# An encoder trunk on one core: the last two squares of a norm summed by TensorE, the norms' low parts issued one tile later, three weight blocks split earlier

## The chip, the core and the metric

The kernel runs on one core of a Trainium2 chip. The metric is the device time of one execution in microseconds. The median of three runs of the kernel before is 2935.86 us, from 2931.73 to 2937.4.

## What is computed

Two layers of an encoder on 1280 tokens of 1024 channels: layer 0 mixes tokens by grouped-query attention, layer 1 by a convolution module; each is followed by a SwiGLU feed-forward network (FFN) of width 2816. Every part starts with a norm and ends with an addition to `x`. Cut to what matters here, everything in float32:

```
def _rms_norm(x, g):
    y = x * lax.rsqrt(jnp.mean(x * x, axis=-1, keepdims=True) + RMS_EPS)
    return y * g

# layer 0
x = x + attention(_rms_norm(x, g_attn)) @ w_o
x = x + (silu(h @ w_gate0) * (h @ w_up0)) @ w_down0        # h = _rms_norm(x, g_ffn0)
# layer 1
u, v = split(_rms_norm(x, g_conv) @ w_in + b_in)
c = depthwise_conv(u * sigmoid(v)) + dw_b                  # width 31, each sequence by itself
x = x + silu(_layer_norm(c, ln_g, ln_b)) @ w_out + b_out
x = x + (silu(h @ w_gate1) * (h @ w_up1)) @ w_down1        # h = _rms_norm(x, g_ffn1)
y = _rms_norm(x, g_final)
```

## The kernel before

**Numbers in two parts.** TensorE (PE) multiplies in a shortened float32. Each float32 operand is therefore split into a high part, a cast on ScalarE (ACT, L133), and a low part, source minus high part, on VectorE (DVE, L134); a product is three matmuls, high by high, high by low and low by high. Weights come by DMA into `raw` (four buffers) and are split into `hl` (five buffers) by `weights` (L140) or, for the FFNs computed with seven products for a 2 by 2 block in place of eight, by `seven`. Such an FFN has `two_blocks` (L732 on) with the products y, z, v and x, whose operands `norm7` (L683) makes: from the normed tiles k and k + 4 the differences `t1` to `t4` (`t12`, `t34`, L718 to L721), and of those the split pairs `b` (`cut7`, L701; `b1` in `seven_right`).

**Layout.** Activations lie with channels on the partitions, in 8 tiles of 128 (NK = 8), and tokens along the free axis. The tokens are worked off in two halves: HA (0 to 639) and HB (640 to 1279); the convolution cuts at 624 (CA, CB).

**Order of the work.** The attention fills the first 620 us. Behind it PE's queue is written out by hand: `drive(main, bg, rate)` lets the main generator run one step, then the background generator `rate` steps, and so on. The stages are: w_o of HA; w_o of HB blocks 0 to 4, beside norm7 of HA for FFN0; FFN0 HA; w_o of HB blocks 5 to 7, beside the norm of HA for the convolution; conv_in HA, beside norm7 of HB and the depthwise convolution (on DVE); FFN0 HB; conv_out CA, beside the norm of HB; conv_in HB, beside the norm of CA; FFN1 CA (in groups of blocks); conv_out CB; the last group of FFN1 CA, beside norm7 of CB; FFN1 CB; the close with the final norm. The orders of DVE, ACT, GpSimd (POOL) and SyncE (SP, which issues the loads) are made by a scheduler from the order of the code and estimated readiness; each engine works its queue off strictly in order, so an instruction that waits holds up all behind it.

**A norm.** For each of the eight tiles `Total.add` squares `x` on ACT into `sq` (L633, three buffers) and POOL adds it to the running sum (L637). `factors` lets PE multiply the sum by a column of ones, `st` (L652): eight matmuls of 80 or 82 tokens by one column for the norms of a token half, six of 104 for CA and for the final norm. DVE forms the reciprocal root in a chain of tiny operations from `rs_w` (L107) to `rs_r` (L128). `spread` broadcasts it over the partitions with PE, `bc` (L661). Then `norm` (L674) scales each tile into `hf` on DVE and splits it into `hn`, tile by tile; `norm7` scales at L692. `pause(k)` between `factors` and the norm puts k steps of the background between them, and with that one or more PE blocks of the main generator between `st` and `bc`.

**Lines that the prediction uses.** `wo` (L614) are the matmuls of a w_o block, `x<-wo` (L794) the addition behind it on DVE; `pd` those of an FFN's down projection; `ci` (L941) those of conv_in; y, z, v, x the seven products (L728 to L730); `r<-y` (L744) copies on ACT of one of them; L1055 the loads for the final norm.

Of the kernel before, what the change touches and what calls it, by code (L numbers as in the profile page):

```python
# [10 lines left out]
F32 = mybir.dt.float32  # L11
F32R = mybir.dt.float32r
I32 = mybir.dt.int32
AF = mybir.ActivationFunctionType
ALU = mybir.AluOpType
# [4 lines left out]
P = 128  # L20
D = 1024
NK = D // P
# [47 lines left out]
def trunk(ctx: ExitStack, tc: tile.TileContext, a: dict):  # L70
# [24 lines left out]
    def col(ct, r):  # L95
        return cols[:, ct, r:r + 1]
# [35 lines left out]
    def split(dst_h, dst_l, src):  # L132
        S.copy(out=dst_h, in_=src)  # L133
        V.tensor_tensor(out=dst_l, in0=src, in1=dst_h.bitcast(F32), op=ALU.subtract)  # L134
# [281 lines left out]
    with tc.tile_pool(name="at", bufs=1, reuse_waits="tile") as at, \  # L416
# [33 lines left out]
        class Unit:  # L450
            def __init__(self, spec):
                self.j, self.qt0, self.nq, self.kt0, self.nk, self.h = spec
                self.g = self.j // 2
                self.w = self.nk * P
                self.s, self.nm, self.l, self.p, self.pt = {}, {}, {}, {}, {}
                self.o = None

                heads = (0, 1) if self.h is None else (self.h,)
                tiles = [(h, i) for h in heads for i in range(self.nq)]
                per = 1024 // self.w  # L460
                self.tiles = [tiles[i:i + per] for i in range(0, len(tiles), per)]
# [131 lines left out]
    def slot(name, dt=F32):  # L593
        return sp.tile([P, SLOT], dt, tag="s", name=name)
# [4 lines left out]
    def acc(name):  # L599
        return pp.tile([P, 2, 512], F32, tag="acc", name=name)  # L600

    def two(t, half):
        return t[:, :half.len].rearrange("p (c n) -> p c n", c=2)
# [18 lines left out]
    def hl_pair(name):  # L622
        return slot(name + "h", F32R), slot(name + "l", F32R)

    class Total:


        def __init__(self, ln):
            self.ln, self.tot = ln, None

        def add(self, x):
            new = sp.tile([P, SLOT], F32, tag="sq", bufs=SQUARES, name="sq")[:, :self.ln]
            S.activation(out=new, in_=x[:, :self.ln], func=AF.Square)  # L633
            if self.tot is None:
                self.tot = new
            else:
                GP.tensor_tensor(out=self.tot, in0=self.tot, in1=new, op=ALU.add)  # L637

    def stats(xs, half, eps, box, wait=2):

# [5 lines left out]
        yield from factors(tot, half, eps, box)  # L646

    def factors(tot, half, eps, box):
        tot = getattr(tot, "tot", tot)
        st = acc("st")[:, 0, :half.nst]  # L650
        for j in range(half.nst):
            PE.matmul(st[:half.w, j:j + 1], tot[:, j * half.w:(j + 1) * half.w], ones, start=True, stop=True)  # L652
        box.append(rsqrt(st[:half.w, :], (half.w, half.nst), 1.0 / D, eps))
        yield

    def spread(r, half):

        bc = acc("bc")
        for j in range(half.nst):
            c, i = divmod(j, half.per)  # L660
            PE.matmul(bc[:, c, i * half.w:(i + 1) * half.w], r[:, j:j + 1].to_broadcast([half.w, P]),  # L661
                      ident[:half.w, :half.w], start=True, stop=True)
        return bc[:, :, :half.n]

    def norm(xs, half, row, out, box=None):

        if box is None:
            box = []
            yield from stats(xs, half, RMS_EPS, box)
            yield  # L670
        bc = spread(box[0], half)
        for ct in range(NK):
            f = slot("hf")
            V.scalar_tensor_tensor(out=two(f, half), in0=two(xs[ct], half), scalar=col(ct, row), in1=bc,  # L674
                                   op0=ALU.mult, op1=ALU.mult)
            h, l = hl_pair("hn")
            split(h[:, :half.len], l[:, :half.len], f[:, :half.len])
            out.append((h, l))
            yield

    def norm7(half, row, ops, load, box, later=None):

        n = half.n
        bc = spread(box[0], half)
        for k in range(NK // 2):
            f = []
            for ct in (k, k + NK // 2):
                x = load(ct)  # L690
                f.append(slot("hf"))
                V.scalar_tensor_tensor(out=two(f[-1], half), in0=two(x, half), scalar=col(ct, row), in1=bc,  # L692
                                       op0=ALU.mult, op1=ALU.mult)
                yield
            sums = seven_right(f[0][:, :n], f[0][:, n:2 * n], f[1], n, ops)
            for pair, x in sums:
                if later is None:
                    cut7(ops, n, pair, x)
                else:
                    later.append((pair, x))  # L700
            yield  # L701

    def cut7(ops, n, pair, x):
        h, l = hl_pair("b")
        split(h[:, :2 * n], l[:, :2 * n], x[:, :2 * n])
        for i, c in zip(pair, (slice(0, n), slice(n, 2 * n))):
            ops[i].append((h[:, c], l[:, c]))

    def seven_right(b11, b12, low, n, ops):


        b21, b22 = low[:, :n], low[:, n:2 * n]
        t12, t34 = slot("t12"), slot("t34")
        t1, t2, t3, t4 = t12[:, :n], t12[:, n:2 * n], t34[:, :n], t34[:, n:2 * n]
        p1 = slot("b1", F32R)
        split(p1[:, :n], p1[:, n:2 * n], b11)
        ops[1].append((p1[:, :n], p1[:, n:2 * n]))
        V.tensor_tensor(out=t1, in0=b12, in1=b11, op=ALU.subtract)  # L718
        V.tensor_tensor(out=t2, in0=b22, in1=t1, op=ALU.subtract)
        V.tensor_tensor(out=t3, in0=b22, in1=b12, op=ALU.subtract)  # L720
        V.tensor_tensor(out=t4, in0=b21, in1=t2, op=ALU.subtract)  # L721
        cut7(ops, n, (5, 6), t12)
        return ((7, 4), t34), ((2, 3), low)

    def product(ps, left, right, first):

# [181 lines left out]
    def pause(steps):  # L908
        for _ in range(steps):
            yield  # L910

    def first(*steps):
        for g in steps:
            yield from g
# [257 lines left out]
    with tc.manual_schedule(engines={mybir.EngineType.PE}):  # L1172
        oa, ob, xa, xb, ha, hb = [], [], [], [], sevens(), sevens()
        pairs = groups(*[2] * (FF // P // 2))
        drive(heads(HA, oa))
        box, box_b = [], []
        tot_a = Total(HA.len)
        drive(attn_out(HA, oa, xa, lambda ct, x: tot_a.add(x)), heads(HB, ob))
        tot_b, take_b = taken(HB)
        drive(attn_out(HB, ob, None, take_b, range(5)),  # L1180
              first(factors(tot_a, HA, RMS_EPS, box), pause(3), norm7(HA, R_F0, ha, lambda ct: xa[ct], box)), 4)
        ob = []
        tot_a, take_a = taken(HA)
        drive(ffn(0, ha, xa, HA, pairs, None, lambda ct: take_a(ct, xa[ct])), heads(HB, ob), 2, iter(()))
        hc, u, y, box, box_a = [], [], [], [], []
        drive(attn_out(HB, ob, None, take_b, range(5, NK)),
              first(factors(tot_a, HA, RMS_EPS, box_a), pause(2), norm(xa, HA, R_CONV, hc, box_a)), 3)
        xa, later = [], []
        w = CA.len + GAP
        bg = conv_mid(u, w, box)  # L1190
        drive(conv_in(hc, HA, u),
              both(first(factors(tot_b, HB, RMS_EPS, box_b), pause(2), norm7(HB, R_F0, hb, stored(HB), box_b, later)), bg, RATE0),
              1, finish=False)
        for pair, x in sorted(later, key=lambda p: -p[0][0]):
            cut7(hb, HB.n, pair, x)
        for ct in range(NK):
            xb.append(slot("x"))
            nc.sync.dma_start(xb[ct][:, :HB.len], x_d[ct * P:(ct + 1) * P, HB.lo:HB.hi])
        drive(ffn(0, hb, xb, HB, pairs, load=True), conv_norm(box, w, CA, y), 3, bg, RATE - 1)
        xa, ha, hc = [], [], []  # L1200
        drive(conv_out(y, CA, xa), norm(xb, HB, R_CONV, hc), 2)
        spill(xb, HB)
        u, y, box = [], [], []
        w = CB.len
        bg = conv_mid(u, w, box)
        drive(conv_in(hc, HB, u), both(norm(xa, CA, R_F1, ha), bg, RATE0), 1, finish=False)
        gs = groups(4, 4, 4, 2, 4, 4)
        drive(ffn(1, ha, xa, CA, gs[:-1]), conv_norm(box, w, CB, y), 3, bg, RATE)
        xb, hb, box, rest = [], sevens(), [], []
        drive(conv_out(y, CB, xb))  # L1210
        tot, take = taken(CA)
        drive(ffn(1, ha, xa, CA, gs[-1:], None, lambda ct: take(ct, xa[ct])),
              norm7(CB, R_F1, hb, lambda ct: xb[ct], box), 3, stats(xb, CB, RMS_EPS, box))
        drive(ffn(1, hb, xb, CB, pairs, rest), final(tot, CA))
# [41 lines left out]
```

## Time and profile before

| | |
|---|---|
| median of three runs | 2935.86 us |
| the profiled execution | 2935.9 us |
| its span, first to last instruction | 2934.1 us |
| mean granted clock of TensorE | 0.987 of full speed |
| ACT busy | 40% |
| POOL busy | 16% |
| bytes moved by DMA | 438.69 MB |

The profile is of one execution. Its busy times are those of an engine's datapath; PEld is TensorE's loading of weights, which overlaps the matmuls. Rows of the timeline give the start in us from the span's start, the length, the engine, the line of the kernel, the operation, what is written and what is read, the shapes and a count; in brackets stands how long the engine sat idle before, and whose end released it. A matmul of `st` leaves two rows, as do those of `bc`. Matmuls overlap in the timeline, so that their cost is read from the distance of starts. The granted clock is that which the throttle gave TensorE, 1.00 or 0.50 at any moment here, and a number between them is a mean over a window.

### The profile page before, as it was taken

The page shows a single profiled execution, that of the slowest core. Times are in us where ns is not written, and L with a number is a line of the kernel's source. Part 1 is how long each engine was busy: PE and PEld are TensorE (multiplying, and loading weights), DVE is VectorE, ACT ScalarE, POOL GpSimd, SP SyncE. Part 2 cuts the span into 40 slices and gives each one's busy share as a digit, 9 for nine tenths or more (in the row PEclk, how much of TensorE's full clock was granted, in tenths as well). Part 3 has the DMA queues.
Part 4 walks back from the last instruction along what each step waited for, and adds up shares of the span by engine and source line. Part 5 has one row for each costly group of instructions (what it writes and reads, how often), then busy time and mean ns, then how long its engine had stood idle before and what let it go on. Part 6 is the DMA issues. An engine that isn't in the chain of part 4 may idle for free.

```text
span 2934.1 us, 47020 instructions
## 1 busy us (share of the span) xinstructions
PE 2851.1 (97%) x18573; PEld 2728.0 (93%) x18573; DVE 2281.0 (78%) x3705; ACT 1172.4 (40%) x1853; POOL 469.7 (16%) x453
## 2 busy tenths in 40 slices
PE   8989999999999999999999999999999998999997
PEld 6767888789999999999999999999999998999997
DVE  7988999967777776697998666989984438877776
ACT  4438888864433334222111243222222324333332
POOL 2445555522000001110000213010002011000000
PEclk9999999999999999899999999999999999999999
DMA  4532232146887777357666754333324422422221
GB/s 152 181 123 58 53 90 59 44 119 196 277 280 274 267 265 258 106 180 256 223 244 222 277 182 135 115 105 91 98 91 153 130 77 94 134 87 73 86 72 52
DMA packets 316326, 438.69 MB, mean 150 GB/s; under 512 B 22297, under 2 KB 244513, under 8 KB 299209
## 3 DMA queue, kind: packets, MB, share of 16 engines
q1 hardware_dynamic: 298488, 400.10, 42.5%
q0 software_dynamic: 5280, 21.42, 2.0%
q10 hardware_dynamic: 12336, 14.16, 1.4%
q8 instruction: 146, 2.39, 0.3%
q14 instruction: 76, 0.61, 0.1%
HBM read 299.46 MB, written 130.93 MB: 147 GB/s over the span
## 4 chain that ended last, share of the span: by engine, by line
PE 80%; DVE 13%; DMA 2%; issue 2%; ACT 2%; POOL 1%; DVEq 0%; ACTq 0%; SPq 0%; POOLq 0%
PE pd L614 17%; PE ci L941 8%; PE s L472 4%; PE pt L513 4%; PE co L614 4%; PE pg L614 3%; PE pu L614 3%; DVE c L982 3%; PE z L730 3%; PE z L728 3%; PE z L729 3%; PE v L729 3%; PE v L728 3%; PE v L730 3%; PE y L728 3%; PE wo L614 3%
## 5 line engine op out<-in xcount | busy, mean ns | idle before, releaser
L133 ACT CAST hl<-raw 128x1024 fp32r<-128x1024 f32 x328 | 341.0, 1049 | 691.3 <-issue 333.1
L614 PE MATMUL pd<-hh,hl 128*128 128x320 f32 (+2 forms) x2752 | 523.8, 309 | 0.7 <-DVE x L849 0.7
L134 DVE TENSOR_TENSOR hl<-raw,hl 128x1024 fp32r<-128x1024 f32 x328 | 410.4, 1253 | 139.7 <-ACT hl L133 139.2
L982 DVE SCALAR_TENSOR_TENSOR c<-u,cols,c 128x640 f32<-128x640 f32 (+1 forms) x480 | 429.2, 897 | 8.1
L614 PEld LDWEIGHTS pd<-hh,hl 128*128 128x128 f32 x2752 | 434.1, 188 | 1.2 <-DVE x L849 1.2
L849 DVE TENSOR_TENSOR x<-pd,x 128x640 f32<-128x640 f32 (+2 forms) x304 | 248.4, 821 | 118.3 <-PE pd L614 116.4
L614 PE MATMUL pd<-hl 128*128 128x320 f32 (+2 forms) x1376 | 313.9, 309 | 0.0
L637 POOL TENSOR_TENSOR sq<-sq 128x640 f32<-128x640 f32 (+2 forms) x63 | 120.5, 1913 | 847.2 <-ACT sq L633 846.3
L614 PEld LDWEIGHTS pd<-hl 128*128 128x128 f32 x1376 | 230.6, 188 | 0.0
L941 PE MATMUL ci<-hnh,hl 128*128 128x320 f32 (+2 forms) x1024 | 198.6, 314 | 1.2 <-ACT hnh L133 0.9
L484 DVE TENSOR_SCALAR_CACHE_REDUCE s<-s,r_q 128x1024 f32<-128x1024 f32 (+1 forms) x160 | 181.1, 1132 | 23.4 <-PE s L472 16.9
L134 DVE TENSOR_TENSOR pl<-pt,ph 128x512 fp32r<-128x512 f32 x272 | 186.8, 687 | 15.2 <-ACT ph L133 10.5
L506 POOL TENSOR_SCALAR p<-p,rl 128x1024 f32<-128x1024 f32 (+1 forms) x160 | 158.2, 992 | 170.5 <-DVE rl L503 130.3
L513 PEld LDWEIGHTS pt<-ident,p 128*128 128x128 f32 x1088 | 132.3, 141 | 52.7 <-DVE pl L134 17.0
L133 ACT CAST ph<-pt 128x512 fp32r<-128x512 f32 x272 | 159.5, 589 | 48.5 <-PE pt L513 41.2
L728 PE MATMUL z<-bh,hl 128*128 128x320 f32 (+1 forms) x528 | 166.2, 315 | 11.7 <-DMA hl<-w_w_up 5.2
L513 PE MATMUL pt<-ident,p 128*128 128x128 f32 x1088 | 166.2, 275 | 7.6 <-DVE pl L134 4.3
L941 PEld LDWEIGHTS ci<-hnh,hl 128*128 128x128 f32 x1024 | 168.2, 192 | 3.1 <-ACT hnh L133 3.1
L730 PE MATMUL z<-bh,hl 128*128 128x320 f32 (+1 forms) x528 | 166.4, 315 | 1.4 <-DVE hl L134 1.4
L729 PE MATMUL z<-bl,hl 128*128 128x320 f32 (+1 forms) x528 | 166.2, 315 | 0.0
L495 ACT ACTIVATE p<-s,nm 128x1024 f32<-128x1024 f32 (+1 forms) x160 | 159.2, 998 | 10.9 <-DVE s L484 7.5
L614 PE MATMUL pu<-hnh,hl 128*128 128x312 f32 x704 | 133.6, 307 | 0.0
(238 smaller groups left out, 6809.2 us busy)
## 6 DMA issues: line engine op xcount, KB each, us to landing
raw<-in_w_down_dram SPq DMA_DIRECT2D x88, 512.0 KB
raw<-in_w_gate_dram SPq DMA_DIRECT2D x66, 512.0 KB
raw<-in_w_up_dram SPq DMA_DIRECT2D x66, 512.0 KB
w_w_gate<-hl SPq DMA_DIRECT2D x33, 1024.0 KB
w_w_up<-hl SPq DMA_DIRECT2D x33, 1024.0 KB
hl<-w_w_gate SPq DMA_DIRECT2D x33, 1024.0 KB
hl<-w_w_up SPq DMA_DIRECT2D x33, 1024.0 KB
raw<-in_conv_w_in_dram SPq DMA_DIRECT2D x32, 512.0 KB
```

The source lines that it names most:

```text
L133: S.copy(out=dst_h, in_=src)
L134: V.tensor_tensor(out=dst_l, in0=src, in1=dst_h.bitcast(F32), op=ALU.subtract)
L484: V.tensor_scalar(out=s[:, c], in0=s[:, c], scalar1=r_q[self.j // 4][b][:, i, head:head + 1], scalar2=None, op0=ALU.mult, op1=ALU.min, acc ...
L495: S.activation(out=p[:, c], in_=s[:, c], func=AF.Exp, bias=nm[:, i:i + 1], scale=-1.0, accum_out=l[:, i:i + 1])
L513: PE.transpose(ps[:, n * P:(n + 1) * P], self.p[n][:, kt * P:(kt + 1) * P], ident)
L614: PE.matmul(ps[:, c, :n], wt, x[:, c * n:(c + 1) * n], start=first and k == 0 and not end and xi == 0, stop=last and k == nk - 1 and end)
L728: PE.matmul(ps, wh, h, start=first and k == 0, stop=False, skip_group_check=True)
L729: PE.matmul(ps, wh, l, start=False, stop=False, skip_group_check=True)
L730: PE.matmul(ps, wl, h, start=False, stop=k == len(right) - 1, skip_group_check=True)
L849: V.tensor_tensor(out=two(xs[ct], half), in0=pd[:, :, :n], in1=two(xs[ct], half), op=ALU.add)
L941: PE.matmul(ps[:, c, :hi - lo], wt, x[:, lo:hi], start=k == 0 and not end and xi == 0, stop=k == NK - 1 and end)
L982: V.scalar_tensor_tensor(out=c[:, :ln], in0=u[:, k:k + ln], scalar=col(ct, R_DW + k), in1=c[:, :ln], op0=ALU.mult, op1=ALU.add)
```

## The change

Five edits, line numbers of the new kernel in brackets:

- `Total` keeps the sum of squares 0 to 5, still added up by POOL, and gives squares 6 and 7 slots of their own. `factors` multiplies all three parts by the ones and lets PE add them up in PSUM: 24 matmuls for 8, and 18 for 6 (`st`, L657). This touches all nine norms that are made in this way.
- `norm` and `norm7` issue the low part of a split one tile (of norm7: one tile pair) later: `high` (L695) issues the cast and returns the subtraction (L696) as a function that is called after the next tile's scaling (`hf`, L682 and L710). In `seven_right` `t1` and `t2` come ahead of the split of `b1`.
- While the last down projection of FFN0 HA runs, `ending` calls `weights` for three w_o blocks of HB (5, 6 and 7) after its tiles 1, 3 and 5; `attn_out` takes them from `w_a`, as it already did for earlier blocks.
- The pause before the norm of HA for the convolution is 1 for 2.
- The `later` operands of norm7 of HB are cast first, all of them, and then subtracted.

```diff
     class Total:
         def __init__(self, ln):
-            self.ln, self.tot = ln, None
+            self.ln, self.parts, self.count = ln, [], 0
 
         def add(self, x):
-            new = sp.tile([P, SLOT], F32, tag="sq", bufs=SQUARES, name="sq")[:, :self.ln]
-            S.activation(out=new, in_=x[:, :self.ln], func=AF.Square)
-            if self.tot is None:
-                self.tot = new
+            self.count += 1
+            late = self.count > NK - 2
+            new = slot("sq") if late else sp.tile([P, SLOT], F32, tag="sq", bufs=SQUARES, name="sq")
+            S.activation(out=new[:, :self.ln], in_=x[:, :self.ln], func=AF.Square)
+            if late or not self.parts:
+                self.parts.append(new)
             else:
-                GP.tensor_tensor(out=self.tot, in0=self.tot, in1=new, op=ALU.add)
+                tot = self.parts[0][:, :self.ln]
+                GP.tensor_tensor(out=tot, in0=tot, in1=new[:, :self.ln], op=ALU.add)
...
     def factors(tot, half, eps, box):
-        tot = getattr(tot, "tot", tot)
         st = acc("st")[:, 0, :half.nst]
+        m = len(tot.parts) - 1
         for j in range(half.nst):
-            PE.matmul(st[:half.w, j:j + 1], tot[:, j * half.w:(j + 1) * half.w], ones, start=True, stop=True)
+            for i, part in enumerate(tot.parts):
+                PE.matmul(st[:half.w, j:j + 1], part[:, j * half.w:(j + 1) * half.w], ones, start=i == 0, stop=i == m)
...
     def norm(xs, half, row, out, box=None):
...
-        for ct in range(NK):
-            f = slot("hf")
-            V.scalar_tensor_tensor(out=two(f, half), in0=two(xs[ct], half), scalar=col(ct, row), in1=bc,
-                                   op0=ALU.mult, op1=ALU.mult)
-            h, l = hl_pair("hn")
-            split(h[:, :half.len], l[:, :half.len], f[:, :half.len])
-            out.append((h, l))
-            yield
+        past = None
+        for ct in range(NK + 1):
+            now = None
+            if ct < NK:
+                f = slot("hf")
+                V.scalar_tensor_tensor(out=two(f, half), in0=two(xs[ct], half), scalar=col(ct, row), in1=bc,
+                                       op0=ALU.mult, op1=ALU.mult)
+                h, l = hl_pair("hn")
+                now = high(h[:, :half.len], l[:, :half.len], f[:, :half.len])
+                out.append((h, l))
+            if past is not None:
+                past()
+            past = now
+            if ct < NK:
+                yield
+
+    def high(h, l, x):
+        S.copy(out=h, in_=x)
+        return lambda: V.tensor_tensor(out=l, in0=x, in1=h.bitcast(F32), op=ALU.subtract)
...
     def norm7(half, row, ops, load, box, later=None):
...
-            sums = seven_right(f[0][:, :n], f[0][:, n:2 * n], f[1], n, ops)
-            for pair, x in sums:
-                if later is None:
-                    cut7(ops, n, pair, x)
-                else:
-                    later.append((pair, x))
-            yield
+            for low in past:
+                low()
+            past = seven_right(f[0][:, :n], f[0][:, n:2 * n], f[1], n, ops, later)
+            yield
+        for low in past:
+            low()
...
+        def ending(ct):
+            take_a(ct, xa[ct])
+            if ct in (1, 3, 5):
+                c = slice((5 + ct // 2) * P, (6 + ct // 2) * P)
+                w_a.append(weights(a["w_o"][0][:, c].rearrange("(k p) c -> p k c", p=P)))
+
+        drive(ffn(0, ha, xa, HA, pairs, None, ending), heads(HB, ob), 2, iter(()))
...
-              first(factors(tot_a, HA, RMS_EPS, box_a), pause(2), norm(xa, HA, R_CONV, hc, box_a)), 3)
+              first(factors(tot_a, HA, RMS_EPS, box_a), pause(1), norm(xa, HA, R_CONV, hc, box_a)), 3)
```

PE's queue where the norm of HA for the convolution meets w_o blocks 5 and 6 of HB (`wo`): before, a whole block stands between `st` and `bc`; the rows left out are the rest of that block.

```order
L614 MATMUL wo<-ol,hl 128x320 x2
L614 MATMUL wo<-oh,hl 128x320 x2
L652 MATMUL st<-ones,sq 80x1 x8
L614 MATMUL wo<-oh,hl 128x320 x2
L614 MATMUL wo<-ol,hl 128x320 x2
...
L614 MATMUL wo<-oh,hl 128x320 x2
L661 MATMUL bc<-ident,rs_r 128x80 x8
L614 MATMUL wo<-oh,hl 128x320 x2
```

The same place after:

```order
L614 MATMUL wo<-ol,hl 128x320 x2
L614 MATMUL wo<-oh,hl 128x320 x2
L657 MATMUL st<-ones,sq 80x1 x24
L666 MATMUL bc<-ident,rs_r 128x80 x8
L614 MATMUL wo<-oh,hl 128x320 x2
```

`st` has three times as many matmuls, and `bc` stands directly behind it. Apart from the `st` at the eight other places, which have grown in the same way, PE's order is the same.

DVE's queue in norm7 of HA for FFN0, beside w_o of HB, from the first tile pair on (`t12`, `t34` the differences, `b1` and `bl` low parts, `x_` with `wo_` the addition behind w_o block 2), before:

```order
L692 SCALAR_TENSOR_TENSOR hf_8542<-x_7846,cols_105,bc_8533 128x640
L692 SCALAR_TENSOR_TENSOR hf_8544<-x_8140,cols_105,bc_8533 128x640
L134 TENSOR_TENSOR b1_8548<-hf_8542,b1_8548 128x320
L718 TENSOR_TENSOR t12_8546<-hf_8542 128x320
L720 TENSOR_TENSOR t34_8547<-hf_8544,hf_8542 128x320
L719 TENSOR_TENSOR t12_8546<-hf_8544,t12_8546 128x320
L721 TENSOR_TENSOR t34_8547<-hf_8544,t12_8546 128x320
L134 TENSOR_TENSOR bl_8556<-t12_8546,bh_8555 128x640
L134 TENSOR_TENSOR bl_8560<-t34_8547,bh_8559 128x640
L134 TENSOR_TENSOR bl_8564<-hf_8544,bh_8563 128x640
L692 SCALAR_TENSOR_TENSOR hf_8567<-x_7915,cols_105,bc_8533 128x640
L794 TENSOR_TENSOR x_8625<-wo_8576,old_8569 128x640
```

The same place after, from the third row of the above on:

```order
L732 TENSOR_TENSOR t12_8560<-hf_8556 128x320
L696 TENSOR_TENSOR b1_8564<-hf_8556,b1_8564 128x320
L733 TENSOR_TENSOR t12_8560<-hf_8558,t12_8560 128x320
L737 TENSOR_TENSOR t34_8561<-hf_8558,hf_8556 128x320
L738 TENSOR_TENSOR t34_8561<-hf_8558,t12_8560 128x320
L710 SCALAR_TENSOR_TENSOR hf_8577<-x_7915,cols_105,bc_8547 128x640
L815 TENSOR_TENSOR x_8635<-wo_8586,old_8579 128x640
L710 SCALAR_TENSOR_TENSOR hf_8641<-x_8215,cols_105,bc_8547 128x640
L696 TENSOR_TENSOR bl_8567<-t12_8560,bh_8566 128x640
L696 TENSOR_TENSOR bl_8572<-t34_8561,bh_8571 128x640
L696 TENSOR_TENSOR bl_8575<-hf_8558,bh_8574 128x640
```

The three low parts `bl` have moved behind the next pair's two scalings and behind the addition of w_o block 2.

DVE's queue in the norm of HA for the convolution, from the end of the root's chain on (`hnl` the low parts, `hl` that of a weight), before:

```order
L794 TENSOR_TENSOR x_13232<-wo_13183,old_13176 128x640
L134 TENSOR_TENSOR hl_13572<-raw_13570,hl_13572 128x1024
L674 SCALAR_TENSOR_TENSOR hf_13247<-x_7846,cols_105,bc_13238 128x640
L134 TENSOR_TENSOR hnl_13250<-hf_13247,hnh_13249 128x640
L674 SCALAR_TENSOR_TENSOR hf_13253<-x_7915,cols_105,bc_13238 128x640
L134 TENSOR_TENSOR hnl_13256<-hf_13253,hnh_13255 128x640
L674 SCALAR_TENSOR_TENSOR hf_13259<-x_7990,cols_105,bc_13238 128x640
L134 TENSOR_TENSOR hnl_13262<-hf_13259,hnh_13261 128x640
```

And after:

```order
L682 SCALAR_TENSOR_TENSOR hf_13223<-x_7846,cols_105,bc_13214 128x640
L815 TENSOR_TENSOR x_13279<-wo_13230,old_13228 128x640
L682 SCALAR_TENSOR_TENSOR hf_13284<-x_7915,cols_105,bc_13214 128x640
L134 TENSOR_TENSOR hl_13614<-raw_13612,hl_13614 128x1024
L696 TENSOR_TENSOR hnl_13226<-hf_13223,hnh_13225 128x640
L682 SCALAR_TENSOR_TENSOR hf_13290<-x_7990,cols_105,bc_13214 128x640
L696 TENSOR_TENSOR hnl_13287<-hf_13284,hnh_13286 128x640
L682 SCALAR_TENSOR_TENSOR hf_13296<-x_8065,cols_105,bc_13214 128x640
```

A tile's low part now stands behind the scaling of the next tile, and the first scaling ahead of the addition of a w_o block. In SP's queue the loads of the three w_o blocks stand where they stood.

More of the change, by code (lines that the diff above doesn't have):

```diff
@@ L686, in norm7 @@
         bc = spread(box[0], half)
+        past = []
         for k in range(NK // 2):
@@ L694, in norm7, with seven_right @@
                 yield
-            sums = seven_right(f[0][:, :n], f[0][:, n:2 * n], f[1], n, ops)
-            for pair, x in sums:
-                if later is None:
-                    cut7(ops, n, pair, x)
-                else:
-                    later.append((pair, x))
+            for low in past:
+                low()
+            past = seven_right(f[0][:, :n], f[0][:, n:2 * n], f[1], n, ops, later)
             yield
+        for low in past:
+            low()
     def cut7(ops, n, pair, x):
         h, l = hl_pair("b")
-        split(h[:, :2 * n], l[:, :2 * n], x[:, :2 * n])
         for i, c in zip(pair, (slice(0, n), slice(n, 2 * n))):
             ops[i].append((h[:, c], l[:, c]))
-    def seven_right(b11, b12, low, n, ops):
+        return high(h[:, :2 * n], l[:, :2 * n], x[:, :2 * n])
+    def seven_right(b11, b12, low, n, ops, later):
         b21, b22 = low[:, :n], low[:, n:2 * n]
@@ L714, in seven_right @@
         t1, t2, t3, t4 = t12[:, :n], t12[:, n:2 * n], t34[:, :n], t34[:, n:2 * n]
-        p1 = slot("b1", F32R)
-        split(p1[:, :n], p1[:, n:2 * n], b11)
-        ops[1].append((p1[:, :n], p1[:, n:2 * n]))
         V.tensor_tensor(out=t1, in0=b12, in1=b11, op=ALU.subtract)
         V.tensor_tensor(out=t2, in0=b22, in1=t1, op=ALU.subtract)
+        p1 = slot("b1", F32R)
+        ops[1].append((p1[:, :n], p1[:, n:2 * n]))
+        lows = [high(p1[:, :n], p1[:, n:2 * n], b11), cut7(ops, n, (5, 6), t12)]
         V.tensor_tensor(out=t3, in0=b22, in1=b12, op=ALU.subtract)
         V.tensor_tensor(out=t4, in0=b21, in1=t2, op=ALU.subtract)
-        cut7(ops, n, (5, 6), t12)
-        return ((7, 4), t34), ((2, 3), low)
+        for pair, x in (((7, 4), t34), ((2, 3), low)):
+            if later is None:
+                lows.append(cut7(ops, n, pair, x))
+            else:
+                later.append((pair, x))
+        return lows
     def product(ps, left, right, first):
@@ L1183, in trunk @@
         tot_a, take_a = taken(HA)
-        drive(ffn(0, ha, xa, HA, pairs, None, lambda ct: take_a(ct, xa[ct])), heads(HB, ob), 2, iter(()))
+        def ending(ct):
[4 more added lines that the diff above has]
+        drive(ffn(0, ha, xa, HA, pairs, None, ending), heads(HB, ob), 2, iter(()))
         hc, u, y, box, box_a = [], [], [], [], []
         drive(attn_out(HB, ob, None, take_b, range(5, NK)),
-              first(factors(tot_a, HA, RMS_EPS, box_a), pause(2), norm(xa, HA, R_CONV, hc, box_a)), 3)
+              first(factors(tot_a, HA, RMS_EPS, box_a), pause(1), norm(xa, HA, R_CONV, hc, box_a)), 3)
         xa, later = [], []
@@ L1193, in trunk @@
               1, finish=False)
-        for pair, x in sorted(later, key=lambda p: -p[0][0]):
-            cut7(hb, HB.n, pair, x)
+        for low in [cut7(hb, HB.n, pair, x) for pair, x in sorted(later, key=lambda p: -p[0][0])]:
+            low()
         for ct in range(NK):
```

## The prediction

> **What bounds the kernel now.** The page comes first: TensorE (PE) is busy for 97% of the span, so the time is PE's work plus the few places where it idles or runs at a low clock.
>
> ```profile
> PE 2851.1 (97%) x18573; PEld 2728.0 (93%) x18573; DVE 2281.0 (78%) x3705; ACT 1172.4 (40%) x1853; POOL 469.7 (16%) x453
> ```
>
> The view of waits on PE names who ends its idle times (total, times, longest). The third row is what the longer `st` is meant for; the first and the fourth are the norm7 operands; the second, a DMA, isn't touched.
>
> ```profile
> PE y L728 <- ACT b L133: 5.5, 2, 3.8
> PE z L728 <- DMA hl<-w_w_up: 5.2, 1, 5.2
> PE st L652 <- POOL sq L637: 4.3, 2, 2.9
> PE z L728 <- ACT hl L133: 3.7, 1, 3.7
> ```
>
> The view of windows over the five places that the change touches (length, then busy time of PE, PEld, DVE, ACT, POOL, then granted clock, DMA share, GB/s). In order: FFN0 HA's start beside norm7; the `st` behind w_o block 4 of HB; conv_in HA's start behind norm HA; the `st` of norm CA; FFN1 CB's start.
>
> ```profile
> 724.00:740.00 16.00, 11.61 (x58) 10.47 (x57) 14.37 (x24) 7.90 (x12) 6.57 (x2) 0.79 0.62 217
> 1160.00:1172.00 12.00, 9.13 (x60) 8.88 (x60) 5.43 (x7) 5.78 (x7) 5.61 (x4) 0.86 0.40 137
> 1186.00:1210.00 24.00, 20.92 (x88) 17.29 (x87) 15.07 (x27) 7.72 (x9) 2.43 (x3) 0.64 0.26 68
> 2220.00:2240.00 20.00, 18.56 (x127) 18.30 (x126) 14.49 (x26) 3.06 (x4) 5.79 (x5) 0.91 0.53 171
> 2450.00:2480.00 30.00, 22.25 (x126) 20.81 (x126) 27.13 (x37) 15.66 (x22) 6.85 (x4) 0.83 0.39 122
> ```
>
> What PE loses in a row is its idle time plus the clock's shortfall times the length: 4.4 + 0.21 × 16 = 7.8; 2.9 + 1.7 = 4.6; 3.1 + 8.6 = 11.7; 1.4 + 1.8 = 3.2; 7.8 + 5.1 = 12.9. That is 40.2 us: the most that the edits can win.
>
> **The sum of squares: more PE work at nine places.** The timeline shows an `st` and the matmul behind it (start, length, ... x rows; a matmul of this form leaves two rows), for a norm 80 tokens wide and for a conv norm 104 wide.
>
> ```profile
> 692.51 1.24 PE L652 MATMUL st<-ones,sq 128*80 128x1 f32 x16
> 693.61 0.54 PE L614 MATMUL wo<-oh,hl 128*128 128x320 f32 x2
> 2479.53 1.17 PE L652 MATMUL st<-ones,sq 128*104 128x1 f32 x12
> 2480.57 0.40 PE L728 MATMUL y<-b,hl 128*128 128x328 f32 x1
> ```
>
> Eight matmuls take between 1.10 us (to the next start) and 1.24 (their length): I take 1.15; the six wide ones between 1.04 and 1.17: 1.10. Three parts take three times as long, so the addition is twice that: seven places × 2.3 = 16.1 and two × 2.2 = 4.4, together **+20.6** (the bounds are 19.6 and 22.0). PE is busy in front of and behind all nine, so nothing hides it. POOL loses 18 additions; it is 16% busy, and they count only where `st` waited for them.
>
> **What three parts do to the clock.** PE alone, in stretches on the 3.41 us grid on which the clock changes (length, busy, granted clock, DMA share, GB/s):
>
> ```profile
> 692.00:695.41 3.41, 3.41 (x33) 1.00 0.36 133
> 1659.63:1663.04 3.41, 1.68 (x12) 1.00 0.85 348
> 1663.04:1666.45 3.41, 3.04 (x21) 1.00 0.88 284
> 2226.24:2229.65 3.41, 1.97 (x22) 1.00 0.89 279
> 2229.65:2233.06 3.41, 3.41 (x15) 0.50 0.43 114
> 1202.24:1205.65 3.41, 3.41 (x22) 0.50 0.02 5
> 2228.14 1.33 PE L652 MATMUL st<-ones,sq 128*82 128x1 f32 x16 [1.44 <-POOL sq L637]
> 1202.47 2.21 PE L652 MATMUL st<-ones,sq 128*80 128x1 f32 x16
> ```
>
> The first row holds an `st` of today's length and keeps its clock. A stretch with 1.68 busy keeps the clock; one with 1.97 busy, of which the `st` (seventh row) is about 1.2, loses it. So `st` rows don't seem to count as work: without them that stretch has 0.8 us. The sixth row says the same: PE is busy throughout, 2.2 us of it `st`, and the stretch doesn't raise the clock for the rest. An `st` of 3.45 us covers most of one stretch wherever it falls: the uncovered part drops below 0.8 us at about half of the positions, and below 1.68 at nearly all. I take three in four. One stretch at 0.50 loses half of 3.41: 1.7. At the six places that keep the clock today: 6 × 0.75 × 1.7 = **+7.7** (0 if `st` does count, 20.5 if each drop lasts two stretches).
>
> The Trainium skill, "TensorE: Matmul & The Clock Gate", section "HAM oscillation — how this bites in real kernels", gives the rule "no PE-idle gaps >~3.4µs". By that rule a busy `st` drops nothing, and the sum would be 7.7 us lower; the trace disagrees, since a wait of 1.44 us with an `st` behind it was enough at 2226.
>
> **Waits that go, and what is late next.** Squares 6 and 7 no longer pass through POOL. At 2228.14 the wait of 1.44 goes, with a little of its low clock: **−1.6**.
>
> ```profile
> 1160.83 1.57 POOL L637 TENSOR_TENSOR sq<-sq 128x640 f32<-128x640 f32 x1 [0.85 <-ACT sq L633]
> 1162.43 0.74 ACT L633 ACTIVATE sq<-x 128x640 f32<-128x640 f32 x1 [1.68 <-POOL sq L637]
> 1167.24 1.58 PE L652 MATMUL st<-ones,sq 128*80 128x1 f32 x16 [2.87 <-POOL sq L637]
> 1204.72 0.16 DVE L107 TENSOR_SCALAR rs_w<-st 80x8 f32<-80x8 f32 x1 [3.53 <-PE st L652]
> 1207.92 0.16 DVE L128 SCALAR_TENSOR_TENSOR rs_r<-rs_t,rs_r 80x8 f32<-80x8 f32 x1
> 1195.55 0.83 DVE L134 TENSOR_TENSOR hnl<-hf,hnh 128x640 fp32r<-128x640 f32 x1 [0.79 <-ACT hnh L133]
> 1197.95 0.82 DVE L134 TENSOR_TENSOR hnl<-hf,hnh 128x640 fp32r<-128x640 f32 x1 [0.79 <-ACT hnh L133]
> ```
>
> At 1167.24 the sums come one after the other (1.57 after a square of 0.74). With the sixth addition over at 1162.4 and the last square free of POOL's buffers, `st` starts when w_o is through, 2.87 earlier. But with one pause less, `bc` stands directly behind `st`: all of PE's queue, w_o blocks 6 and 7 and conv_in, waits for the reciprocal root, whose chain on DVE takes 3.36 us from the fourth to the fifth row (a w_o subtraction in it would make it 5). That idle time costs a stretch at half clock, 1.7. In return norm HA's tiles no longer wait for their own cast: the last two rows show one tile per 2.40 us, 0.79 of it waiting; all eight pace conv_in's first part, 8 × 0.79 = 6.3. Sum: −2.87 + 3.36 + 1.7 − 6.3 = **−4.1** (from +2.2, if PE was paced by the clock alone, to −8.5, if DVE's chain finds cover).
>
> **FFN0 HA's start (724).** DVE is 14.37 of 16 busy there, so a reordered DVE queue counts one to one.
>
> ```profile
> 707.23 1.56 DVE L134 TENSOR_TENSOR bl<-t,bh 128x640 fp32r<-128x640 f32 x2 [0.27 <-ACT bh L133]
> 709.45 0.87 DVE L692 SCALAR_TENSOR_TENSOR hf<-x,cols,bc 128x640 f32<-128x640 f32 x1
> 710.24 0.82 DVE L794 TENSOR_TENSOR x<-wo,old 128x640 f32<-128x640 f32 x1
> 709.77 1.05 ACT L133 CAST hl<-raw 128x1024 fp32r<-128x1024 f32 x1 [1.31 <-PE wo L614]
> 736.62 0.39 PE L728 MATMUL x<-bh,hl 128*128 128x320 f32 x1 [0.51 <-DVE x L794]
> ```
>
> In the new DVE order the addition `x<-wo` stands ahead of the three low parts of the first tile pair, and PE's w_o block ends only at about 709.7 (fourth row, a cast that waits for the same block). Before, DVE spent the time from 707.23 on the low parts (first row), ahead of the addition; now it idles some 2.2 us there, and by my walk along the new order some 1.4 more behind a weight's low part whose cast is late. Nothing gives that back, since PE still waits for DVE in the last row, at 736.62: **+3.5** (0 to +7.8).
>
> **FFN1 CB's start (2450).** PE's `z` waits for the weight's low part on DVE and starts again at 2466.39.
>
> ```profile
> 2462.98 1.04 ACT L133 CAST hl<-raw 128x1024 fp32r<-128x1024 f32 x1
> 2466.39 0.64 PE L730 MATMUL z<-bh,hl 128*128 128x328 f32 x1 [1.40 <-DVE hl L134]
> 1669.87 0.74 ACT L633 ACTIVATE sq<-c 128x640 f32<-128x640 f32 x1
> 1670.52 0.41 ACT L744 COPY r<-y 128x320 f32<-128x320 f32 x1
> ```
>
> Now that cast (first row) and its partner stand ahead of the operand's, and DVE takes the weight's low parts before the last `bl`s: `z` could go at 2463.4 or so, 3.0 earlier; less half a microsecond for POOL still adding there: **−2.5** (0 to −12.9). In FFN0 HB the two last squares now stand together on ACT, one of 0.74 ahead of the copy of `r` (rows three and four): **+0.7**.
>
> **At nothing.** The w_o weights issued early: SP's queue has their loads where they stood, behind the same raw buffers, and only their casts could move. `cut7` of `later`: DVE and ACT work beside the FFN's matmuls, hidden by them; without that cover the eight low parts come up to eight casts of 0.74 late. The two squares' own slots: 0 to 1 us if a slot were missing.
>
> **Sum.** 20.6 + 7.7 − 1.6 − 4.1 + 3.5 − 2.5 + 0.7 = +24.3. The profiled execution took 2935.9 with its span of 2934.1, and the median of the three runs is 2935.86, so both give **2960**.
>
> **The rivals.** (1) The clock holds at the six places: 2960 − 7.7 = 2952. For it: an `st` as it is drops no clock at six of nine places. Against: the stretch at 2226. By the quoted rule of the skill it would come out so. (2) The other side: the reordered norms keep DVE from waiting for ACT, so that PE never starves at the five places, and the clock holds there. All 40.2 go: 2935.9 + 20.6 − 40.2 = 2916. It decides as soon as 20.6 + 5.9 = 26.5 of the 40.2 go with the clock held, or 34 with the drops. For it: 0.79 idle per tile. Against: DVE is itself full in the windows at 724 and 2450, and an order of its queue gives it no time. (3) Half of the 40.2 goes and the clock holds: 2935.9 + 20.6 − 20.1 = 2936. (4) Each drop lasts two stretches, as with 6.83 us at 727.79 today: 20.5 in place of 7.7, 2973.
>
> ```profile
> 727.79:734.62 6.83, 5.62 (x19) 0.50 0.32 116
> ```
>
> That the w_o edit does nothing is already in the sum; the other edits are in the order of the queues.
>
> **The numbers.** What a measurement can tell from no change is about 0.2%, 5.9 us. Chances: the forecast 0.53, (1) 0.15, (2) 0.09, (3) 0.11, (4) 0.12. Slower is the forecast with (1) and (4): 0.80; same 0.11; faster 0.09. The range 2940 to 2976 takes in (1), (4) and the bounds of the terms; it leaves out (2) and the lower part of (3).
>
> **What would show it.** Nine `st` of 3.3 to 3.6 us (408 rows where there were 136); stretches of clock 0.50 behind most of those at 692, 1687, 1773, 1838, 2390 and 2480; no wait of `st` for POOL; a wait of `bc` for `rs_r` of 3 to 5 us near 1170; norm tiles every 1.6 us; x of FFN0 HA some 3.5 us later against its block's start. The forecast is wrong if `st` takes far less than three times as long, if the clock stays at 1.00 behind it, or if PE's losses at 724, 1186 and 2450 shrink by over 26 us.

## The result, and the profile after

The changed kernel takes 2965.44 us (median of four runs, 2956.74 to 2968.06) against 2936.63 for the kernel before: 1.0095 times as long, 95% interval 1.007 to 1.012. It is slower by 28.8 us, by the interval 21 to 35; 2960, or +24.3, was forecast.

The page of the changed kernel (busy time, share of the span, instructions): PE is busy for 28.0 us more with 272 more rows, POOL for 33.4 us less; DVE and ACT have nearly what they had.

```profile
PE 2879.1 (97%) x18845; PEld 2759.8 (93%) x18845; DVE 2275.1 (77%) x3705; ACT 1171.2 (40%) x1853; POOL 436.3 (15%) x435
```

The waits of its PE (total, times, longest). No `st` waits for POOL any more. In its place `y` waits for the low part of `b1` (first row), at FFN0 HA's and FFN1 CB's start, and `bc` waits for the root.

```profile
PE y L750 <- DVE b L696: 10.3, 3, 4.0
PE y L749 <- ACT b L695: 5.4, 2, 3.0
...
PE bc L666 <- DVE rs_r L128: 3.6, 1, 3.6
...
PE z L749 <- DMA hl<-w_w_gate: 3.0, 1, 3.0
```

An `st` of the new kernel, and the stretches of low clock behind five of the six `st` that had none before (length, PE busy, granted clock, DMA share, GB/s). 48 rows take 3.83 us to the next matmul here, since their last part already runs at the low clock; where the clock is full they take 3.4 (third and fourth row).

```profile
1693.64 3.97 PE L657 MATMUL st<-ones,sq 128*80 128x1 f32 x48
1697.47 0.88 PE L614 MATMUL pd<-hh,hl 128*128 128x320 f32 x2
...
691.49 3.53 PE L657 MATMUL st<-ones,sq 128*80 128x1 f32 x48
694.89 0.54 PE L614 MATMUL wo<-oh,hl 128*128 128x320 f32 x2
```

```profile
1696.53:1703.36 6.83, 6.83 (x31) 0.50 0.00 0
1788.69:1792.10 3.41, 3.41 (x15) 0.50 0.17 44
1856.95:1863.78 6.83, 6.83 (x31) 0.50 0.24 69
2416.74:2420.15 3.41, 3.41 (x16) 0.50 0.15 10
2508.90:2515.73 6.83, 6.83 (x28) 0.50 0.01 2
```

PE is busy all through them, so that busy time does not show this loss; the granted clock does. They are eight stretches of 3.41 us at half speed, 27.3 us, a loss of 13.7.

Where the time went is read from the same matmul in both traces. The lag is its start after less its start before; the profiled executions took 2935.9 and 2966.58.

| up to (start before, start after) | lag | step | forecast |
|---|---|---|---|
| first `st` (692.51, 691.49) | -1.0 | | |
| first y of FFN0 HA (723.64, 725.00) | 1.4 | +2.4 | 2.3 rows + 1.3 clock |
| its first x (736.62, 742.66) | 6.0 | +4.7 | +3.5 |
| a y of FFN0 HB (1313.95, 1320.54) | 6.6 | +0.5 | -4.1 + 2 × 2.3 rows = +0.5 |
| a v of it (1584.42, 1588.95) | 4.5 | -2.1 | 0 |
| a y of it, behind `st` (1691.59, 1703.72) | 12.1 | +7.6 | 2.3 + 1.3 + 0.7 = 4.3 |
| conv_in HB (1817.47, 1833.45) | 16.0 | +3.9 | 2.3 + 1.3 |
| a `pg` of FFN1 CA (1932.61, 1953.86) | 21.3 | +5.3 | 2.2 + 1.3 |
| a `pg` behind the `st` of CB (2241.29, 2263.37) | 22.1 | +0.8 | 2.3 - 1.6 |
| a `pg` behind the next (2398.16, 2424.62) | 26.5 | +4.4 | 2.3 + 1.3 |
| a v of FFN1 CB (2484.25, 2516.07) | 31.8 | +5.4 | -2.5 + 2.2 + 1.3 = 1.0 |
| end of the span (2934.1, 2964.8) | 30.7 | -1.1 | 0 |

### The profile page after: what moved, and what is told of

Its sections match the earlier page's. It is cut to its first block, busy times and chain, and to the rows that moved or that the text cites. A ratio compares the mean times of both kernels' runs of the same rounds, so it can differ in the third digit from the quotient of the medians.

```text
span 2964.8 us, 47538 instructions
## 1 busy us (share of the span) xinstructions
PE 2879.1 (97%) x18845; PEld 2759.8 (93%) x18845; DVE 2275.1 (77%) x3705; ACT 1171.2 (40%) x1853; POOL 436.3 (15%) x435
## 4 chain that ended last, share of the span: by engine, by line
PE 88%; DVE 8%; DMA 2%; issue 1%; ACT 1%; POOL 0%; DVEq 0%; ACTq 0%; SPq 0%; POOLq 0%
PE pd L614 19%; PE ci L962 8%; PE pg L614 5%; PE pu L614 5%; PE s L472 4%; PE pt L513 4%; PE co L614 4%; PE wo L614 3%; PE z L751 3%; PE z L749 3%; PE z L750 3%; PE v L749 3%; PE v L750 3%; PE v L751 3%; PE y L749 2%; PE y L750 2%
## 5 line engine op out<-in xcount | busy, mean ns | idle before, releaser
L641 POOL TENSOR_TENSOR sq<-sq 128x640 f32<-128x640 f32 (+2 forms) x45 | 82.6, 1836 | 866.0 <-ACT sq L636 865.4
L134 DVE TENSOR_TENSOR pl<-pt,ph 128x512 fp32r<-128x512 f32 x272 | 186.6, 687 | 15.2 <-ACT ph L133 10.5
```

## The experiments

Two theories stood against each other from the start. In the first, PE pays: the longer `st` costs its rows and the clock. In its rivals the clock doesn't mind `st`, or the reordered norms are what costs, or they gain and the sums hide it.

**The sums alone, and all but the sums.** The first kernel is the one before with the new `Total` and `factors`; the second is the changed one with the old:

```diff
-            for i, part in enumerate(tot.parts):
-                PE.matmul(st[:half.w, j:j + 1], part[:, j * half.w:(j + 1) * half.w], ones, start=i == 0, stop=i == m)
+            PE.matmul(st[:half.w, j:j + 1], tot[:, j * half.w:(j + 1) * half.w], ones, start=True, stop=True)
```

> The kernel before with the three-part sum of squares alone. Theory P (PE pays): 20.6 us of st rows and 7.7 us of low clock behind them, less the two waits for POOL (2.9 and 1.6), plus 0.7 for ACT's squares: +24.5, about 2961. Rival C (the clock does not mind st rows): +16.8, about 2953. Rival Q (the loss comes from the reordered norms): at most +6, below 2943.

> The changed kernel with the sum of squares as it was before (POOL adds all eight, st has 8 matmuls). Theory P: what is left of the change is about +4.7 at the start of FFN0 HA, 0 at the start of FFN1 CB and between -4 and 0 at conv_in HA, so 2935 to 2941, no st of over 1.3 us and no low clock behind one. Rival Q: most of the 29 us stays, above 2955. Rival G (the norms gain and the sums hide it): below 2925.

The sums alone: 2965.26 against 2936.87, ratio 1.0099 (1.0085 to 1.0112), +28.4; four more than expected. All but the sums: 2947.66, ratio 1.0033 (1.0021 to 1.0046), +10.8; above the 2941 expected, though outside the ranges of both rivals. So the sums carry the loss, and the rest is a loss too, not a gain. Against the kernel before, the lag in the second kernel's trace grows by 4.5 us from the first y of FFN0 HA to its first x, as expected, and by 4.1 at FFN1 CB's start (from 2449.96 to 2479.38 of the trace before), where nothing was. The two add up to 39, ten more than the whole change costs. PE's waits without the sums:

```profile
PE y L745 <- DVE b L691: 12.5, 3, 5.7
PE bc L661 <- DVE rs_r L128: 5.9, 1, 5.9
...
PE st L652 <- POOL sq L637: 4.9, 2, 2.8
```

With POOL's sum `st` still waits 2.8 us and then `bc` 5.9 behind it, where the whole change has 3.6 in all (the 4.9 in the last row is the sum of two waits): the edits on that one norm help each other.

**The price of `st` by itself, with thin and with wide matmuls.** The third kernel is the one before with each `st` matmul issued three times on POOL's sum, so that no wait goes. The fourth has, behind each unchanged `st`, 18 matmuls of 256 columns into a bank that nobody reads:

```diff
+        for _ in range(18):
+            PE.matmul(ps[:, 1, :2 * P].rearrange("p (a b) -> p a b", a=2), ident_r, wide, start=True, stop=True)
```

> The kernel before with each st matmul issued three times on the same sum, so that no wait for POOL goes: the price of the longer st by itself. Theory P: 20.6 for the rows and 7.7 for the clock, +28, about 2964, and stretches of clock 0.50 behind four or more of the six st at 692, 1687, 1773, 1838, 2390 and 2480. Rival C: +20.6, about 2957, clock 1.00 there.

> The kernel before with 18 matmuls of 256 columns behind each st, written to a bank that nobody reads: about the time of the added st rows (2.3 us by an estimate from 0.13 us a matmul), but in wide matmuls. Theory P (st rows do not count as work for the clock, wide ones do): +20.7, about 2957, and the clock stays at 1.00 behind the six. Rival C (a busy PE is a busy PE): the same clock as with the st issued thrice.

Thrice: 2975.41, ratio 1.0138 (1.012 to 1.0155), +38.5. Wide: 2958.49, ratio 1.0071 (1.0057 to 1.0085), +21.6. PE's extra work is the same to 3%: at 1786 the wide kernel's `st` and fill take 3.34 us together, and three `st` take 3.39. The 18 wide matmuls take 2.23 us of it, 0.124 each for the 0.13 expected.

```profile
1786.45 1.24 PE L653 MATMUL st<-ones,sq 128*80 128x1 f32 x16
1787.56 2.40 PE L656 MATMUL st<-ident_r 128*128 128x256 f32 x18
1789.79 0.45 PE L614 MATMUL co<-yh,hl 128*128 128x312 f32 x2
```

The clock behind the six `st`, first with wide matmuls, at full clock six times of six:

```profile
698.20:701.61 3.41, 3.41 (x25) 1.00 1.01 367
1701.40:1704.81 3.41, 3.41 (x26) 1.00 0.00 0
1789.90:1793.31 3.41, 3.41 (x26) 1.00 0.71 217
1857.30:1860.71 3.41, 3.41 (x25) 1.00 0.55 154
2415.00:2418.41 3.41, 3.41 (x26) 1.00 0.52 154
2506.40:2509.81 3.41, 3.41 (x25) 1.00 0.02 5
```

Then with `st` issued thrice, low behind four of the six (at 1706 and at 1791 it stayed up):

```profile
697.28:700.69 3.41, 3.41 (x15) 0.50 0.92 333
1706.00:1709.41 3.41, 3.41 (x25) 1.00 0.00 0
1861.23:1868.06 6.83, 6.83 (x31) 0.50 0.24 66
2421.01:2427.84 6.83, 6.83 (x33) 0.50 0.21 59
2516.59:2520.00 3.41, 3.41 (x16) 0.50 0.00 0
```

This settles the clock: equal busy time, and only the thin matmuls lower it. The two kinds differ in more than their columns: a matmul of `st` has operands in full float32 and leaves two rows, a wide one has them in the shortened float32 and leaves one (x16 for 8, x18 for 18). No run separates the two. The wide kernel puts the price of the busy time alone at 21.6, where 20.6 was worked out for the rows. The 17 us between the two kernels fit the clock: their profiled executions lie 11.6 us apart, and the stretches behind the six `st` cost the first 10.2 and the second nothing.

**Twice.** Each `st` matmul issued twice, between the two lengths.

```diff
+            for _ in range(2):
+                PE.matmul(st[:half.w, j:j + 1], tot[:, j * half.w:(j + 1) * half.w], ones, start=True, stop=True)
```

> The kernel before with each st matmul issued twice on the same sum. Rows alone: 10.3 us, half of 20.6. Theory P (a stretch of 3.41 us loses its clock when less than some 0.8 to 1.7 us of it are other work; an st of 2.3 us leaves at least 1.1): between no and four drops at the six places, 2946 to 2955. Rival L (the cost goes with the rows, 38.5 us for three times as many): half of that, 19 us, 2955 to 2957.

2954.96 against 2939.24, ratio 1.0054 (1.004 to 1.0067), +15.7: 10.3 of rows and some 5 of clock. The interval, 12 to 20 us, takes in the 19 of rival L too, so the time alone doesn't decide between them. The trace shows the clock: 32 rows (2.25 us to the next matmul) lower it behind three of the six `st` (the last three rows; the first row is one of the three that held):

```profile
1787.35:1790.76 3.41, 3.41 (x26) 1.00 0.49 147
1851.49:1854.90 3.41, 3.41 (x15) 0.50 0.32 87
2407.87:2411.28 3.41, 3.41 (x15) 0.50 0.23 29
2500.03:2503.44 3.41, 3.41 (x14) 0.50 0.00 0
```

**The norm's later low part, alone and with the shorter pause.** The first kernel is the one before with the new `norm` and nothing else. The second is the changed kernel without the sums and with the old `norm7`; to the first it adds the pause of 1 and the early w_o weights.

```diff
+                now = high(h[:, :half.len], l[:, :half.len], f[:, :half.len])
...
+            if past is not None:
+                past()
+            past = now
```

> The kernel before, with norm alone (not norm7) issuing its low parts one tile later; the pause stays 2, the sums and norm7 as before. Theory H (the half of the change on norm is a gain where the norm paces PE): conv_in HA's start loses some 6 us less, 2930. Rival Z (an order gives DVE no time): 2936 and unchanged. Rival W (a low part now stands behind the addition of w_o block 6 and waits for PE): 2937 to 2942.

> The changed kernel with the sums and norm7 as before: the later low parts of norm, the pause of 1 and the early w_o weights are left. Theory A (norm7's later low parts cost 5 us at the start of FFN0 HA and 5 at the start of FFN1 CB): 10 us less than all but the sums, 2937, y's waits at 725 and 2467 as in the kernel before. Rival B (the missing block between st and bc costs, 6 us of wait there): 2944 or more. It stands beside the run of norm alone: the difference is the price of pause 1 and of the w_o weights, 0 to +8.

Norm alone: 2927.7 against 2936.08, ratio 0.997 (0.996 to 0.998), 8.4 us faster than the kernel before; in the traces 6.6 of it come between 1168.68 and 1210.01. With the pause of 1: 2938.23, ratio 1.0005 (0.9996 to 1.0014). So this edit is a gain where a norm paces PE, and the pause gives all of it back. A kernel with norm's edit and the early w_o weights, and the pause at 2, has in every engine's queue the same rows with the same waits as norm alone, so the w_o weights change nothing and the 10.5 us are the pause's. It wasn't run. DVE's timeline of norm alone at conv_in HA shows a tile every 1.53 us (between starts of `hnl`), with no wait for a cast, where it was 2.40:

```profile
1191.95 0.81 DVE L691 TENSOR_TENSOR hnl<-hf,hnh 128x640 fp32r<-128x640 f32 x1
1192.69 0.87 DVE L677 SCALAR_TENSOR_TENSOR hf<-x,cols,bc 128x640 f32<-128x640 f32 x1
1193.48 0.81 DVE L691 TENSOR_TENSOR hnl<-hf,hnh 128x640 fp32r<-128x640 f32 x1
```

And the windows of the same stage (columns as in the windows of before): the clock is 0.93 where it was 0.64, since the low stretch that starts at 1193 lasts 3.41 us and the one before, from 1192, lasted 17.07.

```profile
1180.00:1204.00 24.00, 20.64 (x135) 19.75 (x134) 18.65 (x32) 9.79 (x12) 3.73 (x4) 0.93 0.34 98
```

With the pause of 1 PE's first row of waits is `bc`:

```profile
PE bc L661 <- DVE rs_r L128: 6.3, 1, 6.3
```

**norm7's later low parts.** All but the sums is 10.8 us above the kernel before, and the same with the old `norm7` and the old order of its `later` operands 2.2 (2938.23 against 2936.08): 8.6 us are the price of norm7's edits. The traces agree: with the old `norm7` the two steps of 4.5 and 4.1 us named above are 0.0 and -0.4. Is it only `b1`, which the first product reads? This kernel splits `b1` at once and leaves the other low parts late:

```diff
+            p1 = slot("b1", F32R)
+            split(p1[:, :n], p1[:, n:2 * n], f[0][:, :n])
+            ops[1].append((p1[:, :n], p1[:, n:2 * n]))
             for low in past:
                 low()
```

> All but the sums (POOL adds all squares), with one more edit: norm7 splits b1, which y as the first product reads, at once, and the other low parts stay late. Theory A1 (it is b1 behind the last pair's low parts that FFN0 HA and FFN1 CB wait for): 8 to 10 us less than all but the sums, 2938 to 2940. Rival A2 (the low parts of the differences cost, or the additions of w_o in front of them): within 3 us of 2947.7.

2944.91 against 2936.08, +8.8, ratio 1.0033 (1.0021 to 1.0046), the same ratio as without this edit (+10.8): A2, and above A1's 2940. PE now waits for the cast of `b1`:

```profile
PE y L745 <- ACT b L133: 11.2, 2, 7.5
PE bc L661 <- DVE rs_r L128: 6.1, 1, 6.1
...
PE z L747 <- DVE hl L134: 5.4, 1, 5.4
```

The last pair's scaling itself is late: DVE starts it at 732.43, before at 727.51, with PE's first y 1.3 us later. That the lost DVE time in front of it is the cause, below, is read from the trace and wasn't tried by an edit of its own.

**The sum at two places only.** Norm's later low part, and the three-part sum only for the norm of HA for the convolution and for the conv norm of CB, where `st` waited for POOL.

```diff
-            late = self.count > NK - 2
+            late = self.count > NK - self.late
...
-        tot_a, take_a = taken(HA)
+        tot_a, take_a = taken(HA, 2)
...
-        bg = conv_mid(u, w, box)
+        bg = conv_mid(u, w, box, 2)
```

> The kernel before, with norm's low parts one tile later and the three-part sum at two of the nine places only: the norm of HA for the convolution and the conv norm of CB, where st waits for POOL (2.9 and 1.4 us). Theory P: each pays 2.3 us of rows for its wait, with a low clock that was there already: about 1 us from the run of norm alone, 2929 to 2932. Rival: each costs 4 or more as elsewhere, 2938.

2927.84, ratio 0.9974 (0.9964 to 0.9984), as good as norm alone (2927.7): there the three parts pay for themselves and no more. Both versions beat both kernels.

**The changed kernel with a pause of 2.**

```diff
-              first(factors(tot_a, HA, RMS_EPS, box_a), pause(1), norm(xa, HA, R_CONV, hc, box_a)), 3)
+              first(factors(tot_a, HA, RMS_EPS, box_a), pause(2), norm(xa, HA, R_CONV, hc, box_a)), 3)
```

> The changed kernel, all of it, with the pause before the norm of HA for the convolution set back to 2, so that a w_o block stands between st and bc again. With POOL's sums the pause of 1 cost 10.5 us (2938.2 against 2927.7). Theory M (with three parts st does not wait for POOL and the chain of the root is disturbed less, 3.6 us of wait for 6.3, so that the pause costs less here): 3 to 7 us less than the changed kernel, 2958 to 2962. Rival S (the same price): 2955. Rival T (the short pause is what the three-part sum needs, and starts the norm earlier): 2965 or more.

2961.71 against 2939.24, ratio 1.0077 (1.0065 to 1.009), +22.5 where the changed kernel has +28.8: 6 us less, as in M, but the intervals of the two ratios overlap, so the times exclude neither S (10.5 less) nor no difference. In the traces the part from 736.62 to 1313.95 costs -7.1 us with the pause of 2 (lag 10.9 to 3.7) and +0.5 with 1.

## Why the prediction was right, point by point

**The sum as a whole.** The steps of the table add up to 31.7 us where 24.3 were forecast, and the medians differ by 28.8. Of the 7.4 too much in the traces, 6.0 are the clock behind the six `st`; the other misses, up and down, nearly cancel, and that is luck.

**The rows of `st`: right.** 48 rows take 3.4 us at full clock, three times the time before; 20.6 forecast (its own terms, 16.1 and 4.4, make 20.5), and 21.6 measured for nearly the same PE time in wide matmuls.

**The clock: right in kind, too small.** The step was "I take three in four. One stretch at 0.50 loses half of 3.41: 1.7." Five drops of six came in the changed kernel, four in the kernel with `st` thrice. The sums alone and the changed kernel with a pause of 2 have four and six, together 19 of 24, so three in four holds. Which places drop is set by where `st` falls on the grid of 3.41 us. Take the share of an `st` in a stretch up to the next matmul's start. Then, at the six places of these four kernels and of `st` twice, the clock fell behind every stretch in which `st` left less than 1.3 us to other matmuls, and behind none in which it left 1.5 or more; at 1.34 to 1.36 it fell once and held twice. The `st` of the changed kernel at 691.49 lies across a border of the grid and leaves 1.9 and 1.5 us, so that the clock held:

```profile
689.60:693.01 3.41, 3.41 (x36) 1.00 0.38 98
693.01:696.42 3.41, 3.41 (x39) 1.00 0.92 287
```

The step that was too small is the length: three of the five drops lasted two stretches, 13.7 us in place of 7.7. The stretches from 1696.53, 1856.95 and 2508.90 start inside an `st` (the first of these ends at 1697.6), have wide matmuls behind it for the rest, 2.3 us in the first, and don't get the clock back; those from 1788.69 and 2416.74 are wide matmuls nearly throughout, and do. The 13.7 lie about half way to rival (4), whose 20.5 takes all six places for two stretches each; at three in four that would have been 15.3. The Trainium skill, "TensorE: Matmul & The Clock Gate", section "HAM oscillation — how this bites in real kernels", gives the rule "no PE-idle gaps >~3.4µs". Here the clock fell though PE was busy without a gap, so the runs with thin and with wide matmuls decide against that rule for thin ones. Rival (1), that the clock holds, falls.

**The norm of HA for the convolution: right.** -4.1 plus the rows of two `st` is +0.5, and +0.5 was measured; the agreement to a tenth is luck, in one pair of traces. The wait for POOL is gone; PE waits for the root:

```profile
1169.93 3.53 PE L657 MATMUL st<-ones,sq 128*80 128x1 f32 x48
1177.05 1.33 PE L666 MATMUL bc<-ident,rs_r 80*128 80x80 f32 x5 [3.58 <-DVE rs_r L128]
```

3.58 us against 3.36 forecast. The low clock behind it costs some 2.0 more than before, for 1.7: it lasts 10.24 us from 1174.29, of which PE idles 2.8, and lasted 3.41 before. The tiles come every 1.5 us, as in norm alone; here DVE first lost 7.98 us behind the addition of w_o block 6, which the order had put ahead of the first low part:

```profile
1180.76 0.88 DVE L682 SCALAR_TENSOR_TENSOR hf<-x,cols,bc 128x640 f32<-128x640 f32 x1 [3.86 <-PE bc L666]
1189.62 0.82 DVE L815 TENSOR_TENSOR x<-wo,old 128x640 f32<-128x640 f32 x1 [7.98 <-PE wo L614]
```

What the prediction didn't see is how much of the gain the pause took: alone, norm's edit brings 8.4 us.

**FFN0 HA's start: right, a little small.** +4.7 for +3.5. DVE's timeline shows the wait worked out from the order, 2.17 us for 2.2:

```profile
708.04 0.87 DVE L710 SCALAR_TENSOR_TENSOR hf<-x,cols,bc 128x640 f32<-128x640 f32 x1
711.08 0.82 DVE L815 TENSOR_TENSOR x<-wo,old 128x640 f32<-128x640 f32 x1 [2.17 <-PE wo L614]
```

What lies behind it, 1.2 us more than forecast, I have not taken apart; the low clock there lasts 10.24 us for 6.83 before.

**FFN1 CB's start: wrong.** The failed step is "`z` could go at 2463.4 or so, 3.0 earlier; less half a microsecond for POOL still adding there: **−2.5**". The gain was nothing: from 2449.96 to the `st` there the lag stays at 26.5. Before, PE idled 7.75 us in that window; now the three waits at `y` and `z` make 7.7:

```profile
2485.41 0.64 PE L749 MATMUL y<-b,hl 128*128 128x328 f32 x1 [2.45 <-ACT b L695]
2489.68 0.64 PE L750 MATMUL y<-b,hl 128*128 128x328 f32 x1 [3.63 <-DVE b L696]
2492.77 0.64 PE L751 MATMUL z<-bh,hl 128*128 128x328 f32 x1 [1.63 <-DVE hl L134]
```

I followed the weight's low part that `z` waits for and not the low part of the last `b1`, which `y` reads before it and which now stands behind three low parts of the pair ahead. A stall went and the operand next in line took its place.

**FFN0 HB, 4.3 forecast, 7.6 measured.** PE's waits from 1584 on were 4.1 us before (for `r`, in two waits) and are 4.8 now, 3.0 of them for a load of `hl<-w_w_gate`. Behind that wait lies a stretch of low clock that wasn't there, and behind the `st` two, not 0.75 of one:

```profile
1669.22:1672.63 3.41, 3.41 (x15) 0.50 0.79 264
```

Of the eleven traces other than that of the kernel before, ten have a low stretch at this place, that of norm alone too (from 1664.01), so it isn't the longer `st` that makes it; why the load came late isn't settled. The -2.1 us ahead of all this has no cause that I can name.

**At nothing: right** for the w_o weights, by the queues. **POOL's waits:** at 2228 +0.8 for the forecast 0.7.

Rivals (2) and (3) fall: of the 40.2 us lost at the five places, the whole change won next to nothing. Without the rows of `st`, the steps there are +4.7, -4.1, -1.5 and 0, about -1 in all. The run of norm alone shows that the mechanism of (2) is real in one place: 8.4 us. Open is why the sums alone and the rest together make ten more than the whole. Over 4 of it is at the norm of HA (from 736.62 to 1313.95 the lag grows by 5.8, -0.8 and 0.5 in the sums alone, the rest and the whole) and some 2 at FFN1 CB's start (-1.7, 4.1 and 0.1); the remainder is within what runs of one kernel differ by, 11 us in the changed one.

## What to carry to other kernels

In these runs a float32 matmul with one column of output cost PE its slot and did not hold the clock up, so a reduction that moves to TensorE to save idle POOL time pays twice, once in rows and once in the stretches behind it; move it only where PE waits anyway. A low part issued one tile later helps where a norm alone paces PE and DVE has idle time between its tiles; where DVE is full, or another addition slips in ahead of the low parts, it costs. When a wait is removed, look for the operand that the consumer reads just before and just after.

## What the runs showed of the hardware

TensorE's granted clock falls to 0.50 behind float32 matmuls of one column though PE is busy without a gap: with an `st` three times as long (3.2 to 3.4 us) at 19 of 24 places, in the four kernels that have one at the six places; twice as long (2.1 to 2.25 us) at three of six; with 18 matmuls of 256 columns behind an `st` of the old length, 3.34 us in all, at none of six. At these places the clock fell behind a stretch of 3.41 us with less than 1.3 us of wide matmuls, and held behind one with 1.5 us or more; in between, both happened. Once low, it came back after one stretch where at least 2.95 us of that stretch were wide matmuls, and only after two where they were 2.7 us or less (22 drops).
